# A two-block transformer layer in float32: GpSimd work, modulation products, transposes and three steps of the second block rearranged

## The chip, the cores and the metric

The kernel runs on one core of a Trainium2 chip. A core has five engines that work side by side, each through its own queue in order: TensorE (PE in the profile; PEld is its weight load), VectorE (DVE), ScalarE (ACT), GpSimd (POOL) and SyncE (SP), which only issues transfers. The metric is the device time of one execution in microseconds (us); lower is better.

## The reference

Batch 1, 512 tokens, width 1024. A first block, then a second, each once; all float32.

```python
def first_block(x, c, ...):
    mod = silu(c) @ w_mod + b_mod                       # 6 x 1024 columns
    sh1, sc1, gt1, sh2, sc2, gt2 = split(mod, 6)
    h = rms_norm(x, g_norm1) * (1 + sc1) + sh1
    q, k, v, ga, gb = split(h @ w_in)                   # 5 x 512 columns
    attn = dilated_attention(q, k, v)                   # 8 heads of 64, softmax
    u = ga * sigmoid(gb)
    y = causal_depthwise_conv(u, conv_w, width=31) + conv_b
    conv = silu(layer_norm(y, conv_ln_g, conv_ln_b))
    x = x + gt1 * (concat(attn, conv) @ w_out)
    h2 = rms_norm(x, g_norm2) * (1 + sc2) + sh2
    x = x + gt2 * hier_moe(h2, ...)                     # 32 experts, top 2 of a group
    return rms_norm(x, g_final)

def second_block(x, meta, ...):                         # 16 meta tokens ahead: 528 rows
    hn = rms_norm(h); sb_q, sb_k, sb_v, g_q, g_k, g_v, g_r, g_lr, merge = split(hn @ w_in)
    sb = stick_breaking(sb_q, sb_k, sb_v)               # 8 heads of 64
    g = log_sigmoid(g_lr @ w_gk_up + b_gk) / 16         # g_lr: 16 columns
    o = rms_norm(gla(g_q, g_k, g_v, g)) * silu(g_r)     # 4 heads, chunked recurrence
    mix = (gate_sb * (sb @ w_sb_out) + gate_gla * (o @ w_gla_out)) @ w_o
    h = h + rms_norm(mix)
    h = h + rms_norm((gelu(conv3(rms_norm(h) @ w_up)) * (rms_norm(h) @ w_gate)) @ w_down)
```

## The kernel before

**Weights.** One stream (`Stream`, L225) brings every weight matrix of both blocks through a plan of units of up to 1 MB, in the order of their use. SP issues a unit's transfer (L271) as soon as one of its `raw` buffers is free: four in the first block until the attention ends, then six more. A buffer is free when its last reader is done with it, and the transfers leave SP in the order of the plan. A unit that is used in the fast product is cast in chunks of 1024 or 512 columns to a high and a low part, `whi` and `wlo` (`split`, L219): ACT rounds the chunk (L220), and VectorE subtracts (L221). For the first 20 chunks (`LOP`, L223 and L479), which are those of `w_gab`, `w_v` and `w_qk`, GpSimd does the subtraction. Three chunks are cast ahead of use. A product of two split operands is three matmuls (`mm3`, L308: L309 to L311).

**Modulation.** The 6144 columns of `mod` come in 24 units of 256 columns (`mod_gen`, L497). A unit's weights lie with the output columns on the partitions, and VectorE multiplies them by silu(c) and sums along the row in one instruction for each 128 columns (L523), two to a unit, then adds `b_mod` (L502). Three units, 15, 21 and 23 (`NMP`), are multiplied on GpSimd (L519), summed by ACT (L507) and get their bias on GpSimd. Units 0 to 7 are used two at a time for the norm of the input (`normed1`, L556), two come after each odd step of the value projection, one after each odd query-key product, four in the attention (`MA`) and four in the output projection.

**First block in order.** (1) The gate projection `pg` with the norm woven in, up to `u = ga * sigmoid(gb)` (L599). (2) The value projection `pv` (L646 to L658), four steps with one chunk each. (3) Eight query-key products `p` (`qk_proj`, L663), the first head pair's attention woven in. (4) Attention over four head pairs (`hp`) of four row blocks (`i`), in a software pipeline: scores `pqk` (L686), bias and maximum on VectorE (L695), exponential on ACT (L699), a diagonal matrix of 1/sum (`dg`, L708, on ACT), a product `pt` of scores and `dg` that transposes and scales at once (L712), its copy `pT` (L720), and the values `pso` (L729), which are split into `mh` and `ml`. (5) All along, VectorE works on the convolution: 120 taps `y = u * w + y` of 128x512 (L633, L635), issued four at a time (`taps`) at a lower priority, so that they stand between the other VectorE work wherever the list scheduler of the framework puts them. Four more taps are products on TensorE (`pe_taps`, `pyt` L859), added by L861. (6) First halves of the output projection `pw` on the attention's half of the rows, the convolution's layer norm (`conv_norm`, `psl`, `psl2`, L824 to L847) woven in, then the second halves on the convolution's rows. (7) Router, and the mixture of experts.

**Second block, the three places.** `proj2_gen` (L1579) multiplies a cast 128-column weight with `nh` and `nl`, the two parts of the normed input, in two column halves of 264. Of `g_lr` only 16 columns exist; their weights come as a 128-column unit, cast like the rest, and make `pl` in 48 matmuls (L1712). In the stick-breaking part (L1745 to L1880) a pipeline of 40 units (4 head pairs `hp`, 5 key blocks `j`, 2 heads `b`) begins with the scores `pz` of one head (`sb_z`, L1783), a contraction over 64 rows of which the other head uses the other 64; it is woven with the query-key projections `pq` (L1587) and the linear attention's levels `pat`. `Sums` (L1612) sums squares over the partitions for the two norms behind: each square is multiplied into one of four 32-row groups of a bank (L1633), ACT copies the bank (L1640), and a second product adds the groups up (L1641).

The order on each engine is made by a list scheduler from the order in which the program is written, with priorities where `high_priority` says so; it was read from the compiled program.

## Time and profile before

| | |
|---|---|
| median of 3 runs | 1839.62 us (1836.7, 1839.62, 1840.88) |
| the profiled execution, its own time | 1838.8 us |
| span of the trace | 1837.0 us, 1.8 us less than its time |
| mean granted TensorE clock | 0.976 of full speed |
| busy in the span: PE, DVE, ACT, POOL | 1752.8, 923.4, 626.5, 180.4 us |
| first block up to the second halves of the output projection | 0 to 257.7 us |
| stick-breaking and linear attention, with their projections | 883 to 1047 us |

A slice of the page's strips is 1/40 of the span, 46 us, and a digit is the busy share in tenths. In the table of windows each row gives, for one stretch, its length and for each engine the busy time and the number of instructions, then the granted clock (1.00 is 2.4 GHz, 0.50 is 1.2 GHz), the share of the 16 transfer engines and GB/s. In the rows by line the numbers behind the bar are the busy time of the group in us, the mean duration of one instruction in ns, and the idle time of the engine just before them with what ended it. An fp32 matmul is two records in the trace, one of split operands is one; matmuls are pipelined, so that the durations of neighbours overlap.

### The profile page before, as it was taken

How to read it: one execution, taken by the hardware profiler on the slowest of the kernel's cores; microseconds unless marked ns; L12 is line 12 of the kernel's file. 1: busy time of each engine (PE TensorE's matmuls, PEld its weight loads, DVE VectorE, ACT ScalarE, POOL GpSimd, SP SyncE). 2: the span in 40 equal slices, each digit the busy share in tenths (PEclk: the TensorE clock that was granted, in tenths of full speed). 3: DMA queues.
4: the chain of work that ended last, by engine and by line, in shares of the span. 5: the costliest groups of instructions: out<-in, count | busy, mean ns of one | idle time of the engine just before them, and what ended most of it. 6: DMA issues, size and time to landing. Idle time of an engine off the chain costs nothing.

```text
span 1837.0 us, 26718 instructions
## 1 busy us (share of the span) xinstructions
PE 1752.8 (95%) x10738; PEld 1264.7 (69%) x10738; DVE 923.4 (50%) x1593; ACT 626.5 (34%) x1146; POOL 180.4 (10%) x162
## 2 busy tenths in 40 slices
PE   6978987999999999999999999999999999999997
PEld 4755754544445444445888768989999799889985
DVE  7999864542424343335577752253331654335534
ACT  3324653211111111104566663252223633223322
POOL 4541020000000000004100000030000111001101
PEclk9998998999999999999999999999999999999998
DMA  8743163899999999941411012113222122232221
GB/s 300 283 165 134 73 231 127 303 409 409 408 411 377 371 407 409 413 166 38 157 63 47 25 38 101 47 50 136 104 95 91 46 92 93 90 105 93 92 86 63
DMA packets 73889, 328.29 MB, mean 179 GB/s; under 512 B 7971, under 2 KB 8227, under 8 KB 59556
## 3 DMA queue, kind: packets, MB, share of 16 engines
q1 hardware_dynamic: 72608, 320.75, 46.3%
q0 software_dynamic: 1152, 5.81, 0.9%
q8 instruction: 85, 1.39, 0.3%
q14 instruction: 40, 0.33, 0.1%
q10 hardware_dynamic: 4, 0.00, 0.0%
HBM read 322.27 MB, written 4.26 MB: 178 GB/s over the span
## 4 chain that ended last, share of the span: by engine, by line
PE 50%; DVE 2%; ACT 1%; POOL 1%; issue 0%; DVEq 0%; ACTq 0%; POOLq 0%
PE p L1609 11%; PE pup L2210 7%; PE pq L1587 6%; PE pg L311 2%; PE pg L309 2%; PE pg L310 2%; PE pd L310 2%; PE pd L311 2%; PE pd L309 2%; PE pz L1789 1%; PE pv L309 1%; PE psb L1870 1%; PE pv L311 1%; PE pv L310 1%; PE pmix L309 1%; PE pmix L310 1%
## 5 line engine op out<-in xcount | busy, mean ns | idle before, releaser
L221 DVE TENSOR_TENSOR wsplit<-raw,wsplit 128x1024 fp32r<-128x1024 f32 (+1 forms) x140 | 166.8, 1194 | 258.5 <-ACT wsplit L220 253.0
L220 ACT ACTIVATE wsplit<-raw 128x1024 fp32r<-128x1024 f32 (+1 forms) x145 | 147.9, 1022 | 261.8 <-PE pd L311 76.4
L1195 PE MATMUL pgu<-raw,x 128*64 128x512 f32 x960 | 220.3, 598 | 0.0
L1195 PEld LDWEIGHTS pgu<-raw,x 128*64 128x64 f32 x960 | 64.1, 136 | 120.0 <-issue 106.9
L1288 DVE SCALAR_TENSOR_TENSOR x<-psx,modc,x 128x512 f32<-128x512 f32 x136 | 93.1, 744 | 48.1 <-PE psx L1296 48.0
L1237 DVE SCALAR_TENSOR_TENSOR yl<-pdn,wsl,yh 128x512 fp32r<-128x512 f32 x34 | 25.4, 751 | 178.8 <-ACT yh L1236 178.4
L1195 PE MATMUL pdn<-raw,hT 128*64 128x512 f32 x480 | 105.7, 593 | 0.7 <-ACT hT L1217 0.7
L635 DVE SCALAR_TENSOR_TENSOR y<-u,cpk,y 128x512 f32<-128x512 f32 x116 | 103.3, 924 | 0.4
L1217 ACT ACTIVATE hT<-pht 128x512 f32<-128x512 f32 x17 | 10.2, 598 | 232.1 <-PE pht L1211 227.5
L1195 PEld LDWEIGHTS pdn<-raw,hT 128*64 128x64 f32 x480 | 34.5, 137 | 69.1 <-issue 64.4
L310 PE MATMUL pd<-wsplit,ah 128*128 128x512 f32 x176 | 71.0, 403 | 2.1 <-DVE wsplit L221 2.0
L1157 PE MATMUL psg<-oh,h2h 128*128 128x256 f32 (+1 forms) x288 | 68.9, 297 | 3.2 <-DVE oh L1142 3.2
L311 PE MATMUL pd<-wsplit,al 128*128 128x512 f32 x176 | 70.0, 398 | 0.0
L309 PE MATMUL pd<-wsplit,ah 128*128 128x512 f32 x176 | 69.1, 398 | 1.0 <-ACT wsplit L220 1.0
L1609 PE MATMUL p<-nha,wsplit 128*128 128x258 f32 x384 | 68.6, 291 | 1.0 <-ACT grb L2059 0.6
L1157 PE MATMUL psg<-oh,h2l 128*128 128x256 f32 (+1 forms) x288 | 65.7, 281 | 0.0
L1609 PE MATMUL p<-nhb,wsplit 128*128 128x258 f32 x384 | 65.5, 282 | 0.0
L221 POOL TENSOR_TENSOR wlo<-raw,whi 128x1024 fp32r<-128x1024 f32 x20 | 59.4, 2982 | 57.7 <-ACT whi L220 47.2
L2210 PE MATMUL pup<-nha,wsplit 128*128 128x258 f32 x352 | 63.9, 290 | 0.9 <-ACT wsplit L220 0.9
L523 DVE CUSTOM_DVE_ANT_0 raw<-raw,h 128x1024 f32<-128x1024 f32 x38 | 62.4, 1668 | 1.1 <-DMA raw<-w_mod 1.1
L1295 PE MATMUL psx<-ohT,yh 128*128 128x512 f32 x136 | 59.3, 436 | 3.3 <-ACT uh L1455 3.0
L2210 PE MATMUL pup<-nhb,wsplit 128*128 128x258 f32 x352 | 61.4, 284 | 0.0
(649 smaller groups left out, 4050.7 us busy)
## 6 DMA issues: line engine op xcount, KB each, us to landing
raw<-w_moe SPq DMA_DIRECT2D x312, 512.0 KB, 10.1
raw<-w_moe SPq DMA_DIRECT2D x36, 1024.0 KB, 8.9
raw<-w_mod SPq DMA_DIRECT2D x24, 1024.0 KB, 6.4
raw<-w_ff SPq DMA_DIRECT2D x22, 1024.0 KB, 4.8
raw<-w_qk SPq DMA_DIRECT2D x12, 1024.0 KB, 4.9
raw<-w_v SPq DMA_DIRECT2D x8, 1024.0 KB, 4.9
raw<-w_mg SPq DMA_DIRECT2D x8, 1024.0 KB, 4.8
raw<-w_fd SPq DMA_DIRECT2D x8, 1024.0 KB, 4.8
```

The costliest lines, as they stand in the source:

```text
L220: act(hi, src, AF.Copy)
L221: return sub(lo, src, hi.bitcast(F32), OP.subtract)
L309: mm(ps, lh, rh, start=first, stop=False)
L310: mm(ps, lh, rl, start=False, stop=False)
L311: mm(ps, ll, rh, start=False, stop=last)
L635: tap[0] = stt(y[:, m, :], src, w, y[:, m, :], OP.mult, OP.add)
L1157: fix(mm(ps[k // 2][:, k % 2 * 256:][:, :n], w[i][:, k * P:(k + 1) * P], oh[:, i, :n], start=(i == 0 and w is h2h and k % 2 == 0), stop=(i ...
L1195: fix(mm(ps[s, :], l[:, s], w[:, 2 * b + i, :], start=first, stop=last, skip_group_check=True))
L1288: stt(xT[m], ps, gt2(m), xT[m], OP.mult, OP.add)
L1587: mm(ps[a], l[:, kk, :], r[kk][:, a * HF:(a + 1) * HF], start=(kk == 0 and fl == 0), stop=(kk == k - 1 and fl == 2))
L1609: mm(ps[a], l[:, kk, :], ends(r[kk])[:, a], start=(kk == 0 and fl == 0), stop=(kk == k - 1 and fl == 2))
L2210: mm(ps[:, a, :HC], l[:, kk, :], x[kk][:, o:o + HC], start=(kk == 0 and fl == 0), stop=(kk == KD - 1 and fl == 2))
```

## The change

In the first block:

- `LOP` goes: all 20 low parts are subtracted on VectorE.
- `NMP` goes: no unit is multiplied on GpSimd, and units 21 and 23 are VectorE's.
- Units 8 to 15 (`MPE`) become products on TensorE. Their weights (`w_modk`) lie with the contraction on the partitions; eight fp32 matmuls of 32 equal columns of silu(c) (`ccols`, made by GpSimd at the start) against 256 columns fill four 32-row groups of a bank, ACT copies them (`evm`), and two matmuls against 1/32 (`part32`) add up groups and copies to a column, to which VectorE adds `b_mod` (`mod_columns`). Four units are used behind the second and four behind the fourth step of the value projection, none in the query-key products. A raw buffer of theirs is free when TensorE has read it.
- `at_transpose`: ACT scales the scores in place by 1/sum, n = 128 to 512 columns, and TensorE transposes them with its transpose operation; `dg` goes.

In the second block:

- `g_lr`: the weights come uncast as 32 columns for each of the 8 row blocks, 32 fp32 matmuls fill four 32-row groups, and `wgk`, zero between its four copies, adds the groups up in the product that follows.
- `sb_z` takes two banks at the first head and issues the scores of both heads behind each other.
- `Sums`: a square is summed by one matmul with 128 columns of ones as soon as the next product is issued; the copy and the second product go.

```diff
...
@@ -287 +288 @@
-                    i = split(hi, lo, src, nc.gpsimd.tensor_tensor if self.nc in LOP else self.lo)
+                    i = split(hi, lo, src, self.lo)
@@ -384,0 +386,7 @@
+    ccol = early.tile([P, KD], F32, name="ccol")
+    act(ccol, cc("c", 0, KD), AF.Silu)
+    ccols = early.tile([P, KD, 32], F32, name="ccols")
+    for k in range(KD):
+        nc.gpsimd.tensor_scalar(ccols[:, k, :], ones[:, 0:32], ccol[:, k:k + 1], None, OP.mult)
+    part32 = early.tile([P, 2], F32, name="part32")
+    nc.vector.memset(part32, 1.0 / 32)
@@ -394 +402 @@
-    NMP = (15, 21, 23)
+    MPE = range(8, 16)
@@ -407 +415 @@
-            add(I["w_mod"][2 * j + h], (2048,), False)
+            add(I["w_modk"][2 * j + h - 12] if 6 <= j < 10 else I["w_mod"][2 * j + h], (2048,), False)
@@ -414 +422 @@
-        add_mod(2)
+        add_mod(4)
@@ -417 +424,0 @@
-        add_mod(1)
...
@@ -499,12 +502 @@
-        late, crow = [], crow_h2
-        def done(c, eng):
-            eng.tensor_tensor(modc[:, c:c + 2], macc[:, c:c + 2], cc("b_mod", c, 2), OP.add)
-        def sums():
-            for raw, c in late:
-                for b in range(2):
-                    act(raw[:, b, :], raw[:, b, :], AF.Copy, accum_out=macc[:, c + b:c + b + 1])
-                done(c, nc.gpsimd)
-            late.clear()
+        crow = crow_h2
@@ -512,3 +503,0 @@
-            with tc.high_priority(offset=-100):
-                sums()
-            raw = ws.nxt(D)
@@ -515,0 +505,14 @@
+            mod_columns()
+            if n in MPE:
+                raw = ws.nxt(256)
+                ps = p1("pmod")
+                for k in range(KD):
+                    g = 32 * (k % 4)
+                    mm(ps[g:g + 32, 0:256], ccols[:, k, :], raw[:, k, :], start=(k < 4), stop=(k >= 4),
+                       skip_group_check=True)
+                ev = big.tile([P, T], F32, name="evm", tag="t512", bufs=2)
+                act(ev[:, 0:256], ps[:, 0:256], AF.Copy)
+                rows_of.append((ps, ev, c))
+                yield
+                continue
+            raw = ws.nxt(D)
@@ -518,8 +521,4 @@
-            if n in NMP:
-                nc.gpsimd.tensor_tensor(raw, raw, crow[:, None, :].to_broadcast([P, 2, D]), OP.mult)
-                late.append((raw, c))
-            else:
-                for b in range(2):
-                    nc.vector.tensor_tensor_reduce(raw[:, b, :], raw[:, b, :], crow, 1.0, 0.0, OP.mult, OP.add,
-                                                   macc[:, c + b:c + b + 1])
-                done(c, nc.vector)
+            for b in range(2):
+                nc.vector.tensor_tensor_reduce(raw[:, b, :], raw[:, b, :], crow, 1.0, 0.0, OP.mult, OP.add,
+                                               macc[:, c + b:c + b + 1])
+            tt(modc[:, c:c + 2], macc[:, c:c + 2], cc("b_mod", c, 2), OP.add)
...
@@ -529,0 +528,11 @@
+    rows_of = []
+    def mod_columns():
+        for ps, ev, c in rows_of:
+            for b in range(2):
+                mm(ps[:, 256 + 2 * b:258 + 2 * b], ev[:, b * P:(b + 1) * P], part32, start=True, stop=True,
+                   skip_group_check=True)
+            tt(modc[:, c:c + 2], ps[:, 256:260:2], cc("b_mod", c, 2), OP.add)
+        rows_of.clear()
@@ -657,2 +666,2 @@
-            next(mod)
-            next(mod)
+            for _ in range(4):
+                next(mod)
@@ -669,2 +677,0 @@
-            if i % 2:
-                next(mod)
@@ -706 +713 @@
-        dg = big.tile([P, 2, P], F32, name="dg", tag="dg", bufs=2)
+        n = (i + 1) * P
@@ -708 +715 @@
-            act(dg[:, b, :], ident, AF.Copy, scale=sm[:, 6 + b:7 + b])
+            act(s[:, b, :n], s[:, b, :n], AF.Copy, scale=sm[:, 6 + b:7 + b])
@@ -712 +719 @@
-                mm(pt[b][:, j * P:(j + 1) * P], s[:, b, j * P:(j + 1) * P], dg[:, b, :], start=True, stop=True)
+                transpose(pt[b][:, j * P:(j + 1) * P], s[:, b, j * P:(j + 1) * P], ident)
...
@@ -1632,3 +1640 @@
-                g, k = self.n[a] % 4, self.n[a]
-                mm(self.ps[a][32 * g:32 * g + 32], ones[:, 0:32], part(sq, a), start=(k < 4), stop=(k >= 4),
-                   skip_group_check=True)
+                mm(self.ps[a], ones, part(sq, a), start=(self.n[a] == 0), stop=(self.n[a] == KD - 1))
@@ -1639,4 +1645 @@
-            ev = t5("ev")
-            act(part(ev, a), self.ps[a], AF.Copy)
-            mm(self.ps[a], ones, part(ev, a), start=True, stop=True)
-            tc.keep_in_program_order(act(part(r, a), self.ps[a], AF.Ln, bias=epsb, scale=1.0 / (32 * count)))
+            tc.keep_in_program_order(act(part(r, a), self.ps[a], AF.Ln, bias=epsb, scale=1.0 / count))
@@ -1712,2 +1715,8 @@
-    for i, _ in enumerate(proj2_gen(KD, nh, nl, pl)):
-        if i == 2:
+    w = ws.nxt(32)
+    for k0 in (0, 4):
+        for x in (nh, nl):
+            for a in range(2):
+                for k in range(4):
+                    mm(pl[a][32 * k:32 * k + 32], w[:, k0 + k, :], x[k0 + k][:, a * HF:(a + 1) * HF].bitcast(F32),
+                       start=(k0 == 0 and x is nh), stop=(k0 > 0 and x is nl), skip_group_check=True)
+        if k0 == 0:
...
@@ -1722,2 +1731,4 @@
-    wgk = cp.tile([16, 512], F32, name="wgk")
-    nc.gpsimd.dma_start(wgk, I["w_gk_up"])
+    wgk = cp.tile([P, 512], F32, name="wgk")
+    nc.gpsimd.memset(wgk, 0.0)
+    for g in range(0, P, 32):
+        nc.gpsimd.dma_start(wgk[g:g + 16], I["w_gk_up"])
@@ -1782,0 +1794,2 @@
+    pz = {}
@@ -1783,0 +1797 @@
@@ -1785,6 +1799,10 @@
-        need(("s", hp))
-        s0, t0, n = SBT[j]
-        ps = p1("pz")
-        r, p = slice(64 * b, 64 * b + 64), sb_keys(j)
-        mm(ps[:p, :n], skh[hp][r, s0:s0 + p], sqh[hp][r, t0:t0 + n], start=True, stop=True)
-        return ps
+        if b == 0:
+            need(("s", hp))
+            s0, t0, n = SBT[j]
+            p = sb_keys(j)
+            for h in range(2):
+                pz[h] = p1("pz")
+            for h in range(2):
+                r = slice(64 * h, 64 * h + 64)
+                mm(pz[h][:p, :n], skh[hp][r, s0:s0 + p], sqh[hp][r, t0:t0 + n], start=True, stop=True)
+        return pz.pop(b)
@@ -2166,0 +2185 @@
+            su.flush(a)
@@ -2169,2 +2187,0 @@
-            if m in (3, 5):
-                su.flush(a)
@@ -2174,0 +2192 @@
+            su.flush(a)
@@ -2196,0 +2215 @@
+            su.flush(a)
@@ -2198 +2217 @@
-            if k % 2:
+            if k == KD - 1:
```

Three places in the order of the engines. The first is SP's queue of weight transfers from the value projection's first unit on (`w_v`, two units; `w_qk`, four; `w_mod` and `w_modk` are modulation units), with what each waits for; before:

```order
L271 DMA raw<-w_v 128x2048 [waits DMAHW7_49,Pool_49]
L271 DMA raw<-w_mod 128x2048 [waits DMAHW0_49,DVE_49]
L271 DMA raw<-w_mod 128x2048 [waits DMAHW1_49,DVE_49]
L271 DMA raw<-w_v 128x2048 [waits DMAHW2_49,Pool_49]
L271 DMA raw<-w_mod 128x2048 [waits DMAHW4_49,DVE_49]
L271 DMA raw<-w_qk 128x2048 [waits DMAHW5_49,DVE_49]
L271 DMA raw<-w_mod 128x2048 [waits DMAHW3_49,Pool_49]
L682 DMA strip<-strip 128x2x512
L271 DMA raw<-w_qk 128x2048 [waits DMAHW7_49,DVE_49]
```

and now:

```order
L272 DMA raw<-w_v 128x2048 [waits DMAHW7_49,DVE_49]
L272 DMA raw<-w_modk 128x2048 [waits DMAHW0_49,DVE_49]
L272 DMA raw<-w_modk 128x2048 [waits DMAHW1_49,DVE_49]
L272 DMA raw<-w_modk 128x2048 [waits DMAHW2_49,DVE_49]
L689 DMA strip<-strip 128x2x512 x2
L272 DMA raw<-w_modk 128x2048 [waits DMAHW3_49,DVE_49]
L272 DMA raw<-w_v 128x2048 [waits DMAHW4_49,PE_49]
L272 DMA raw<-w_modk 128x2048 [waits DMAHW5_49,PE_49]
L272 DMA raw<-w_modk 128x2048 [waits DMAHW6_49,PE_49]
L272 DMA raw<-w_modk 128x2048 [waits DMAHW1_49,PE_49]
L272 DMA raw<-w_modk 128x2048 [waits DMAHW2_49,DVE_49]
L272 DMA raw<-w_qk 128x2048 [waits DMAHW7_49,DMAHW3_49,PE_49]
```

The second `w_v` unit stood two modulation units behind the first and waited for GpSimd; it now stands four behind it and waits for TensorE to have read a modulation unit. The `w_qk` units, of which the last row shows the first, do so too.

The second is VectorE behind the last scores of the attention, up to the sum of the taps from TensorE (L861, now L869): taps (L635, now L644), modulation units (L523, now L522, each with a read of its sum), the last part of the attention (`ml`) and the low parts of the first three `w_out` chunks (`wlo`). Before:

```order
L705 RECIPROCAL sm<-sm 128x2
L635 SCALAR_TENSOR_TENSOR y<-u,cpk_67,y 128x512 x6
L221 TENSOR_TENSOR ml<-pso,mh 128x512
L635 SCALAR_TENSOR_TENSOR y<-u,cpk_67,y 128x512 x3
L221 TENSOR_TENSOR wlo<-raw,whi 128x512
L635 SCALAR_TENSOR_TENSOR y<-u,cpk_67,y 128x512 x3
L221 TENSOR_TENSOR wlo<-raw,whi 128x512
L635 SCALAR_TENSOR_TENSOR y<-u,cpk_67,y 128x512 x2
L221 TENSOR_TENSOR wlo<-raw,whi 128x512
L523 ISA raw,macc<-raw,u 128x1024
L523 ISA macc 128x1
L861 TENSOR_TENSOR y<-pyt,y 128x512
```

and now:

```order
L712 RECIPROCAL sm<-sm 128x2
L524 TENSOR_TENSOR modc<-macc,cpk_67 128x2
L224 TENSOR_TENSOR ml<-pso,mh 128x512
L224 TENSOR_TENSOR wlo<-raw,whi 128x512
L522 ISA raw,macc<-raw,u 128x1024
L522 ISA macc 128x1
L224 TENSOR_TENSOR wlo<-raw,whi 128x512
L522 ISA raw,macc<-raw,u 128x1024
L522 ISA macc 128x1
L224 TENSOR_TENSOR wlo<-raw,whi 128x512
L524 TENSOR_TENSOR modc<-macc,cpk_67 128x2
L869 TENSOR_TENSOR y<-pyt,y 128x512
```

Of 18 taps behind the last scores, the last 14 of which stand in the rows of before, two are left, ahead of the rows of now; two modulation units stand there instead, one ahead of `ml` (its bias is the second row), the other with one instruction ahead of the second low part and one ahead of the third.

The third is TensorE where the scores of the stick-breaking part with 400 columns begin (`pz` from `sqk`; `psb` are values, `pz` from `sp` sums of an earlier unit). Before:

```order
L1870 MATMUL psb<-z,sv 64x16 [waits Activation_49]
L1870 MATMUL psb<-z,sv 64x16
L1837 MATMUL pz<-sp,mtge 128x144 [waits DVE_49]
L1841 MATMUL pz<-sp,mones 128x16
L1789 MATMUL pz<-sqk 128x400 [waits DVE_49]
L1587 MATMUL pq<-nha,wsplit 128x264 x2
```

and now:

```order
L1888 MATMUL psb<-z,sv 64x16
L1855 MATMUL pz<-sp,mtge 128x144
L1859 MATMUL pz<-sp,mones 128x16
L1807 MATMUL pz<-sqk 128x400 [waits Activation_49]
L1807 MATMUL pz<-sqk 128x400 [waits DVE_49]
L1595 MATMUL pq<-nha,wsplit 128x264 x2
```

The two heads' scores stand next to each other, and each waits for its own bank.

## Rows read from the trace of the kernel before

**Rows 1.** The page's strips, 40 slices: busy tenths of PE, granted clock.

```profile
PE   6978987999999999999999999999999999999997
...
PEclk9998998999999999999999999999999999999998
```

**Rows 2.** Windows: start:end, length, PE, PEld, DVE, ACT, POOL, clock, DMA share, GB/s.

```profile
0.00:73.00 73.00, 57.80 (x215) 40.11 (x216) 59.70 (x82) 26.54 (x34) 37.89 (x28) 0.95 0.77 284
73.00:95.40 22.40, 22.40 (x97) 18.02 (x97) 22.37 (x35) 5.14 (x5) 12.47 (x5) 1.00 0.75 281
95.40:165.20 69.80, 55.42 (x222) 41.43 (x222) 69.80 (x108) 21.07 (x43) 22.68 (x8) 0.88 0.47 170
165.20:212.00 46.80, 40.15 (x307) 28.99 (x306) 45.09 (x126) 32.52 (x101) 1.56 (x1) 0.93 0.13 46
...
221.40:257.70 36.30, 29.52 (x108) 19.72 (x108) 30.49 (x39) 17.87 (x29) 9.85 (x4) 0.91 0.73 282
883.00:1047.00 164.00, 162.63 (x1830) 134.52 (x1830) 107.72 (x222) 103.58 (x223) 9.26 (x15) 0.99 0.20 68
```

**Rows 3.** Waits of PE, 0 to 330 us: total, times, longest.

```profile
PE p L309 <- ACT whi L220: 8.9, 1, 8.9
PE psl L824 <- DVE y L861: 6.8, 1, 6.8
...
PE pt L712 <- ACT dg L708: 5.0, 3, 3.7
```

**Rows 4.** The page's groups of instructions, three of them.

```profile
L221 DVE TENSOR_TENSOR wsplit<-raw,wsplit 128x1024 fp32r<-128x1024 f32 (+1 forms) x140 | 166.8, 1194 | 258.5 <-ACT wsplit L220 253.0
...
L221 POOL TENSOR_TENSOR wlo<-raw,whi 128x1024 fp32r<-128x1024 f32 x20 | 59.4, 2982 | 57.7 <-ACT whi L220 47.2
...
L523 DVE CUSTOM_DVE_ANT_0 raw<-raw,h 128x1024 f32<-128x1024 f32 x38 | 62.4, 1668 | 1.1 <-DMA raw<-w_mod 1.1
```

**Rows 5.** Groups of DVE by line: taps at 0 to 138, then at 185 to 222.

```profile
L635 DVE SCALAR_TENSOR_TENSOR y<-u,cpk,y 128x512 f32<-128x512 f32 x36 | 35.8, 1046 | 0.0
...
L635 DVE SCALAR_TENSOR_TENSOR y<-u,cpk,y 128x512 f32<-128x512 f32 x34 | 24.7, 746 | 0.2
```

**Rows 6.** DVE in order of time behind the attention: start, duration, instruction, count.

```profile
215.16 4.67 DVE L635 SCALAR_TENSOR_TENSOR y<-u,cpk,y 128x512 f32<-128x512 f32 x6
...
226.15 6.50 DVE L635 SCALAR_TENSOR_TENSOR y<-u,cpk,y 128x512 f32<-128x512 f32 x3
...
233.17 5.80 DVE L635 SCALAR_TENSOR_TENSOR y<-u,cpk,y 128x512 f32<-128x512 f32 x2
...
240.63 0.68 DVE L861 TENSOR_TENSOR y<-pyt,y 128x512 f32<-128x512 f32 x1
...
243.60 1.21 DVE L523 CUSTOM_DVE_ANT_0 raw<-raw,u 128x1024 f32<-128x1024 f32 x1
```

**Rows 7.** Weight transfers issued at 190 to 262 us: count, KB, us to landing.

```profile
raw<-w_mod SPq DMA_DIRECT2D x3, 1024.0 KB, 7.6
```

**Rows 8.** Weight transfers of the whole execution, from the page: count, KB, us to landing.

```profile
raw<-w_qk SPq DMA_DIRECT2D x12, 1024.0 KB, 4.9
```

**Rows 9.** PE in order of time: a burst of sums of squares, a second product.

```profile
1397.38 1.53 PE L1633 MATMUL psum<-sq,ones 128*32 128x260 f32 x16
...
1420.55 0.67 PE L1641 MATMUL psum<-ev,ones 128*128 128x260 f32 x2
```

**Rows 10.** Groups of ACT by line, 165 to 222 us.

```profile
L720 ACT ACTIVATE pT<-pt 128x384 f32<-128x384 f32 (+3 forms) x28 | 11.9, 445 | 9.3 <-PE pt L712 9.2
L708 ACT ACTIVATE dg<-ident,sm 128x128 f32<-128x128 f32 x26 | 9.0, 393 | 2.4 <-DVE sm L697 1.8 <-DVE sm L705 0.5
```

**Rows 11.** Groups of PE by line: scores at 95 to 222, then at 883 to 1047.

```profile
L686 PE MATMUL pqk<-qk 64*128 64x128 f32 (+3 forms) x64 | 14.0, 494 | 0.0
...
L1789 PE MATMUL pz<-sqk 64*16 64x16 f32 (+4 forms) x62 | 21.2, 421 | 0.6 <-ACT sqk L1758 0.6
```

**Rows 12.** One matmul group of `pl`: durations, first and last start.

```profile
L1587 PE MATMUL pl<-nhb,wsplit x16: 280/284/288, 875.2 to 880.9; 128*128 128x264 f32 x16
```

More of the change, by code (lines that the diff above doesn't have):

```diff
@@ L35 @@
     ("b_mod", 48), ("g_norm1", 8), ("conv_b", 4), ("conv_ln_g", 4), ("conv_ln_b", 4),
-    ("conv_w", 4 * 31), ("g_norm2", 8), ("w_router", 8 * 36),
+    ("conv_w", 4 * 31), ("g_norm2", 8), ("w_router", 8 * 36), ("c", 8),
     ("g_final", 8), ("norm_mix_pre", 8), ("b_gk", 4), ("gla_head_norm", 2),
@@ L67, in pack_inputs @@
     wr = np.concatenate([f("w_router_group")[0], f("w_router_expert")[0]], axis=1)
+    parts["c"] = col(f("c"))
     parts["w_router"] = wr.reshape(8, P, 36).transpose(1, 0, 2).reshape(P, 288)
@@ L97, in pack_inputs @@
         "w_mod": wm.T.reshape(24, 2, P, D).transpose(0, 2, 1, 3).reshape(24, P, 2 * D),
+        "w_modk": np.stack([wm[:, (2 * j + h) * 256:(2 * j + h + 1) * 256].reshape(KD, P, 256).transpose(1, 0, 2)
+                           .reshape(P, 2048) for j in (6, 7, 8, 9) for h in range(2)]),
         "c_row": f("c").reshape(1, D),
@@ L107, in pack_inputs @@
         "w_v2": pair(np.concatenate([rows(w2[:, c:c + 512], 2) for c in (1024, 2560, 3072)])),
-        "w_lr": cols(w2, [4608]),
+        "w_lr": np.pad(w2[:, 4608:4624], ((0, 0), (0, 16))).reshape(KD, P, 32).transpose(1, 0, 2).reshape(1, P, KD * 32),
         "w_qk2": pair(cols(w2, [c + h * P for c, h in (
@@ L221, in split @@
         return sub(lo, src, hi.bitcast(F32), OP.subtract)
-    LOP = []
     class Stream:
@@ L460, in _build @@
     plan += [(I["w_v2"][i], two, "keep") for i in range(2)]
-    plan += [(I["w_lr"][0], (1024,), True)]
+    plan += [(I["w_lr"][0], (KD * 32,), False)]
     plan += [(I["w_qk2"][i], two, True) for i in range(8)]
@@ L476, in _build @@
     ws = Stream(plan, castp, 3, nmoe)
-    for u, (_, sizes, cast) in enumerate(plan[:nmoe]):
-        if cast:
-            LOP.extend(range(ws.first[u], ws.first[u] + len(sizes)))
-    del LOP[20:]
     for h in range(2):
@@ new lines, in mod_gen @@
+        for n, (j, h) in enumerate(mod_order):
+            c = 4 * j + 2 * h
+            mod_columns()
[11 more added lines that the diff above has]
+                continue
@@ L526, in mod_gen @@
+            tt(modc[:, c:c + 2], macc[:, c:c + 2], cc("b_mod", c, 2), OP.add)
             yield
-        sums()
         yield
+    rows_of = []
[6 more added lines that the diff above has]
+        rows_of.clear()
     mod = mod_gen()
@@ L744, in _build @@
     qkp = qk_proj()
-    for _ in range(2):
-        next(qkp)
+    next(qkp)
+    mod_columns()
+    next(qkp)
     wr = lambda k: cc("w_router", 36 * k, 36)
@@ L1711, in _build @@
     pl = [p("pl")[:, :HF] for p in (pns, psx)]
-    for i, _ in enumerate(proj2_gen(KD, nh, nl, pl)):
-        if i == 2:
+    w = ws.nxt(32)
[6 more added lines that the diff above has]
+        if k0 == 0:
             sv_last()
     tc.keep_in_program_order(nc.scalar.preload_act_table_set("natural_log_exp_and_others"))
-    glr = t5("glr", 16)
+    glr = t5("glr")
     for a in range(2):
-        act(glr[:, a * HF:(a + 1) * HF], pl[a][0:16], AF.Copy)
+        act(glr[:, a * HF:(a + 1) * HF], pl[a], AF.Copy)
     ws.lo = tt
```

1 line of the change is left out of this document (removed).

## Prediction

> **What bounds the kernel now.** The page's strips come first: from the seventh slice on PE has nines nearly throughout, so behind 276 us the kernel is PE's work, and only the first six slices, about 276 us, have holes [rows 1]. The windows then cut the first block at the ends of its stages [rows 2]. In 0 to 73 (the gate projection) PE is busy 57.8 of 73.0 us. From 73 on VectorE is the full engine: 22.37 of 22.40 in the value projection, 69.80 of 69.80 in the query-key products, 45.09 of 46.80 until the last scores at 212.0, while PE is busy 55.42 of 69.80 and 40.15 of 46.80 there. The waits of PE name what VectorE and GpSimd hold up: 8.9 us for the cast of a weight, 5.0 for `dg`, and 6.8 behind the attention for the convolution's sum `y` [rows 3]. The granted clock falls to 0.88 and 0.93 in the stretches with those waits. In the second block the place of the change is PE-bound: 162.63 of 164.00 us busy at 883 to 1047, with VectorE at 107.72 and ACT at 103.58 [rows 2], so there each microsecond that PE no longer needs is one of the span, as long as neither fills up.
>
> Times below are of the profiled execution, 1838.8 us, which lies 0.8 under the median of the runs.
>
> **First block, up to the values.** GpSimd took 2.98 us for a low part that VectorE does in 1.19 [rows 4]. In the gate projection the eight low parts come sooner, and PE needs 11.2 us for each of its four steps (half of the value projection's 22.40 us, at full clock, since both have 96 products of 512 columns [rows 2] and a step of `pg` has 48). By the order two of the first four modulation instructions now stand behind the first normed row, which waits for the norm, rather than ahead of it, so the first product comes some 2.7 us later (2 x 1.21 us [rows 6] and a table load), at about 22.7, and four steps with the slow clock at the start end near 71, 2 us earlier than before.
>
> VectorE's account from there to the last scores (139.0 us before): gone are units 8 to 14, seven units of two instructions at 1.668 us [rows 4], 23.4 us, and what taps lose while GpSimd works, 36 x (1.046 - 0.746) = 10.8 us [rows 5]. New are twelve low parts at 1.194, 14.3 us, and 16 taps (18 behind the last scores become 2) at 24.7 / 34 = 0.73, 11.6 us. That is 8.3 us less: if VectorE never waited, the last scores would end at 212.0 - 2 - 8.3, near 201.5.
>
> A rule of the Trainium skill would make that floor lower. The page "SBUF — State Buffer", section "Who interferes with whom", has VectorE and GpSimd share one port pair as an exclusive lock, so that the loser stands still for the whole of the other's instruction; by it all of GpSimd's 12.47 + 22.68 = 35.2 us in these two stretches would come back. The rows show instead that a tap beside GpSimd takes 1.4 times its time [rows 5]. With the rule VectorE would be done so early that PE alone would set the end, which is the second rival below with more chance.
>
> PE's account to the last query-key product (165.2 before): 22.4 + 55.42 x 0.88 = 71.2 us of old work at full clock. The waits for the cast and most of that for `dg` go with GpSimd. New are eight units on PE: eight products of 260 columns in four row groups take 1.53 us [rows 9]; with the two small products and the hand-over to ACT I take 1.9, so 15.2 us (12.2 if all but the burst is hidden, 20 if it waits for ACT in full). New too is that the second value unit and the query-key units can only be fetched when PE has read a modulation unit: the transfer takes 4.9 us [rows 8], cast and low part 2.2 more (the low part may stand behind four taps, 2.9), and three units on PE, 5.7 us, cover it. That leaves 1.4 to 4.3; I take 4 for each of the two places, since a tap is always ready on VectorE. The half clock that follows either costs perhaps 1 to 2 us. From 71: 71 + 71.2 + 15.2 + 8 = 165.4, about 166: **the query-key products gain nothing**, and VectorE waits for them.
>
> **Attention and tail.** Between the last query-key product and the last scores VectorE has five taps fewer by the order (28 for 33 in the last three head pairs), 3.7 us; ACT scales 26 times up to 512 columns where it made 128x128 at 0.393; the nearest row, a copy of the same widths, has 0.445 [rows 10], so ACT's 32.5 of 46.8 us grow by 1.4, or by 4.5 at worst if in place costs as the exponential does, and stay under VectorE. So the last scores come at 166 + 46.8 - 3.7 = 209 to 210, and the last values 8.4 later (9.4 before; the transposes are one record for two), at 218: 3.5 us earlier than before. The tail to the second halves was 36.3 us. Taps beside GpSimd took 6.50 us for three and 5.80 for two there, and `y` was summed only at 240.63 [rows 6]; now two taps stand behind the last scores, so the wait of 6.8 us [rows 3] goes, and of the slow clock (0.91 of 29.5 busy us [rows 2]) 2.7 us. What is late next: unit 21, whose weights are fetched when the attention frees its pool. Three such transfers took 7.6 us in the median, the first of them some 5 [rows 7, 8]. The unit's first instruction now stands ahead of the second chunk's low part, which so comes 5 + 1.2 + 0.7 = 6.9 us after the last values, while PE is through with the first chunk after about 4: a new wait of 3 us (0 to 5). The tail is 36.3 - 6.8 - 2.7 + 3 = 29.8. The second halves start at 218 + 29.8, near 248 for 257.7: **10 us gained in the first block**. This passes on, since the transfers of the experts' weights also start from the pool that the attention frees. Ends: a gain of 21 if VectorE runs to its floor and unit 21 is hidden; a loss of 3 if the units cost 20 us, attention keeps its pace and the wait is 6.
>
> **Second block.** Scores in pairs: the attention's scores have the same form with both heads together: 64 records (32 products of 320 columns on average) in 14.0 us, 1.37 ns a column; the lone scores show 62 of their 80 records in 21.2 us, so 27.4 for 40 products of 269 columns on average, 2.55 ns a column [rows 11]. At the pairs' rate they take 14.7 us, 12.7 less. Each pair now needs two banks at once and by the order waits for ACT and VectorE there, so I take **11.5**, with 8 and 14 as ends. VectorE, at 107.72 of what would be 152 us, doesn't fill up. `g_lr`: 48 products from 873.7 to 881.2, 7.5 us (a quarter of them starts in 875.2 to 880.9 [rows 12]); now four bursts of eight, 4 x 1.53 = 6.1 [rows 9], and no cast on ACT and GpSimd ahead: **2**, ends 0 and 3.5, because the input's last parts arrive when they do. `Sums`: four copies and four second products of 0.67 us [rows 9] go, half of them in a chain that PE waits for, some 3 us; squares that stood in bursts of four groups now cost a full-width product each, where the bursts were few: **2**, ends -2 and 4. Together 15.5, with 8 and 20 as ends.
>
> Sum: 1838.8 - 10 - 15.5 = 1813.3.
>
> **The rivals.** *First: the first block gains nothing.* PE is behind VectorE once the units are on it, and each wait is followed by half clock (0.88 where it waits now [rows 2]). The query-key products then end near 172, attention follows, and the tail only gets back what they lost: 1838.8 - 15.5 = 1823. For it speaks that PE's sum, 165.4, has no slack against 165.2; against it, that 14.4 us of idle PE time stand in the window now. *Second: VectorE's floor.* If low parts are seldom behind taps, the two waits shrink to 1.4, the last scores come near 202 and the gain is 20: 1803. *Third, slower: the clock.* PE's old work from 73 to 257.7 is about 144 us at full clock (the busy times of rows 2 times their clocks, with 8.5 at 212 to 221.4). Now about 12 us of it are lost at half clock. More and shorter pauses (units that wait for ACT, transposes half as long) could leave PE at 1.2 GHz through most of the attention; each microsecond of work there costs another. It decides from 12 + 25.5 = 38 us of work at half clock on; at 50 the time is 1838.8 - 25.5 + 50 - 12 = 1851. Against it: the attention's window is at 0.93 now with the same small products. *Fourth: pairs don't run side by side*, because the second waits for its bank. Then the second block gives 4, the sum is 1825; with the first rival too, 1835.
>
> **How the numbers follow.** Forecast 0.57 (1804 to 1821), first rival 0.17 (1819 to 1829), second 0.13 (1797 to 1805), fourth 0.05 (1821 to 1828), first and fourth together 0.03 (1831 to 1838), slower 0.05. The time is the forecast's, 1813. The range leaves out the slower case, the double one and the lower half of the second: 1800 to 1828. A measurement of this kernel tells about 0.2%, 3.7 us, from no change: faster 0.91, within it 0.04 (most of the double case and of the small losses), slower 0.05.
>
> **What would show it.** Right: no tensor work on POOL at 73 to 258; taps at 0.75 us throughout; waits of PE of about 4 us ahead of the fifth chunk half of `pv` and of the first `p`; the last scores at 205 to 213; no wait of `psl` for `y`, but one of `pw` for a low part; second halves at 244 to 252; a pair of 512-column scores in about 1.1 us and the stretch from 883 shorter by 8 to 14. Wrong: `p` ending after 170, clock under 0.8 in the attention, waits of `pz` for ACT above 0.3 us each.

## The result

The changed kernel takes 1823.82 us in the median of five runs (1819.1 to 1827.15), before 1839.53; the ratio is 0.9918, with a 95% interval of 0.9902 to 0.9934. That is 15.7 us (12 to 18) less, where 25.5 were forecast (1813) and the range went to 1828. The traced run took 1819.83 us, near the lower end of the five, with a span of 1818.0 for 1837.0, so that the two traces differ by 19.0 us, 3 more than the medians. Of those 19.0 the first products of the experts (`psg`) come 11.2 us earlier, and the rest lies in the second block.

### The profile page after: what moved, and what is told of

Read it like the earlier page. It is cut to its first block, busy times and chain, and to the rows that moved or that the text cites. A ratio compares the mean times of both kernels' runs of the same rounds, so it can differ in the third digit from the quotient of the medians.

```text
span 1818.0 us, 26874 instructions
## 1 busy us (share of the span) xinstructions
PE 1740.4 (96%) x10826; PEld 1258.9 (69%) x10826; DVE 882.1 (49%) x1597; ACT 628.6 (35%) x1141; POOL 109.9 (6%) x147
## 4 chain that ended last, share of the span: by engine, by line
PE 48%; DVE 4%; ACT 2%; DMA 1%; POOL 1%; issue 0%; DVEq 0%; ACTq 0%; POOLq 0%
PE p L1617 11%; PE pup L2229 7%; PE pq L1595 4%; PE pg L312 2%; PE pg L310 2%; PE pg L311 2%; PE pd L311 2%; PE pd L312 2%; PE pd L310 2%; PE pv L310 1%; PE pv L312 1%; PE pv L311 1%; PE pmix L310 1%; PE pmix L312 1%; PE pmix L311 1%; PE psb L1888 1%
## 5 line engine op out<-in xcount | busy, mean ns | idle before, releaser
L644 DVE SCALAR_TENSOR_TENSOR y<-u,cpk,y 128x512 f32<-128x512 f32 x116 | 81.4, 750 | 0.1
L1165 PEld LDWEIGHTS psg<-oh,h2h 128*128 128x128 f32 x288 | 54.0, 198 | 9.7 <-issue 5.7
L1617 PEld LDWEIGHTS p<-nha,wsplit 128*128 128x128 f32 x384 | 56.3, 195 | 3.0 <-ACT wsplit L223 0.9
```

What stands on the lines that cost most here:

```text
L644: tap[0] = stt(y[:, m, :], src, w, y[:, m, :], OP.mult, OP.add)
L1165: fix(mm(ps[k // 2][:, k % 2 * 256:][:, :n], w[i][:, k * P:(k + 1) * P], oh[:, i, :n], start=(i == 0 and w is h2h and k % 2 == 0), stop=(i ...
L1617: mm(ps[a], l[:, kk, :], ends(r[kk])[:, a], start=(kk == 0 and fl == 0), stop=(kk == k - 1 and fl == 2))
```

## The profile after

The windows of [rows 2], with the same cuts and columns, in the changed kernel:

```profile
0.00:73.00 73.00, 59.35 (x224) 41.46 (x225) 49.11 (x100) 31.87 (x41) 12.27 (x26) 1.00 0.81 299
73.00:95.40 22.40, 18.04 (x125) 12.53 (x124) 18.38 (x32) 3.54 (x6) 0.00 (x0) 0.93 0.49 184
95.40:165.20 69.80, 66.09 (x319) 48.56 (x318) 61.71 (x111) 24.33 (x46) 2.30 (x2) 0.92 0.53 186
165.20:212.00 46.80, 41.34 (x276) 25.32 (x274) 42.52 (x121) 37.46 (x104) 0.00 (x0) 0.96 0.14 46
212.00:221.40 9.40, 7.86 (x62) 6.42 (x63) 2.78 (x7) 4.80 (x11) 0.00 (x0) 1.00 0.48 143
221.40:257.70 36.30, 36.30 (x142) 24.02 (x141) 23.55 (x43) 19.28 (x32) 4.64 (x16) 1.00 0.76 304
```

GpSimd (the last of the five busy times) has left 73 to 95 us altogether, but VectorE, full there before, is now idle for 4.0 of 22.40 us, and for 8.1 of the next 69.80. The waits of PE up to 330 us, for [rows 3]:

```profile
PE pmod L534 <- ACT evm L514: 3.2, 7, 0.5
...
PE pva L311 <- DVE wlo L224: 2.3, 1, 2.3
...
PE pt L719 <- ACT s L715: 1.7, 3, 1.1
PE p L312 <- DVE wlo L224: 1.7, 1, 1.7
```

The waits of 8.9 for a cast and 6.8 for `y` are gone. New are those of the units and two for a low part, of the third weight chunk of the values (its first half is the fifth of all halves) and of the first query-key chunk. VectorE's own waits at 71 to 215 us show what it is idle for:

```profile
DVE modc L536 <- PE pmod L534: 10.0, 8, 3.2
```

It stands 10.0 us before the eight additions of `b_mod`, each of which needs a unit's last product from PE. PE in order of time at the first group of four units (start, duration, instruction, records, wait):

```profile
81.98 1.50 PE L511 MATMUL pmod<-raw,ccols 128*32 128x256 f32 x22
83.63 0.61 PE L534 MATMUL pmod<-part,evm 128*128 128x2 f32 x4 [0.15 <-ACT evm L514]
84.17 1.07 PE L511 MATMUL pmod<-raw,ccols 128*32 128x256 f32 x16
85.69 0.61 PE L534 MATMUL pmod<-part,evm 128*128 128x2 f32 x4 [0.45 <-ACT evm L514]
...
91.00 0.50 PE L310 MATMUL pva<-whi,hh 128*128 128x512 f32 x1 [0.45 <-ACT whi L223]
93.98 0.80 PE L311 MATMUL pva<-wlo,hh 128*128 128x512 f32 x1 [2.25 <-DVE wlo L224]
```

Four units take from 81.98 to 90.54, 2.14 us each, and then the next chunk is not cast. Its weights are not what is late: their transfer was issued at 83.19 and took 4.8 us. ACT rounds the chunk right behind the last unit's copy, from 89.89 on, and VectorE, which follows the order of its own queue, subtracts behind three taps:

```profile
90.72 2.06 DVE L644 SCALAR_TENSOR_TENSOR y<-u,cpk,y 128x512 f32<-128x512 f32 x3
92.71 2.36 DVE L224 TENSOR_TENSOR wlo<-raw,whi 128x1024 fp32r<-128x1024 f32 x2
```

The second group, 107.17 to 115.77, ends in the same way. The waits for casts are 2.7 us behind the first group (0.45 and 2.25) and 2.0 behind the second (0.34 and 1.68), and the clock falls behind each. Windows of 10 us of the changed kernel; between 100 and 110 us, and from 130 to 190 us, the clock is 1.00:

```profile
90.00:100.00 10.00, 7.29 (x22) 5.48 (x23) 9.36 (x15) 1.89 (x2) 0.00 (x0) 0.66 0.83 319
110.00:120.00 10.00, 6.43 (x51) 3.23 (x43) 7.18 (x14) 3.98 (x6) 0.67 (x1) 0.82 0.99 383
120.00:130.00 10.00, 10.00 (x37) 8.02 (x38) 8.91 (x12) 1.55 (x2) 0.00 (x0) 0.84 0.40 134
```

PE is busy for some 10.5 us at 1.2 GHz there, so about half of that, 5.3 us, is lost (an estimate from these records). The query-key products end at 169.9, for 165.2 before; the last scores at 210.1, for 212.0; the last values at 219.0, and the second halves begin at 246.5, for 257.7.

## The experiments

Each is the changed kernel but for its edit, if nothing else is said, and is compared by its ratio to the kernel before; a difference of two such ratios is known to about 0.25%, 4 to 5 us.

**The two halves apart.** `first_only` has the second block of before, `second_only` the first block of before.

> The change's first-block half alone, the second block as before. Prediction's sum: 10 us less than before. By the two traces (the experts' first products came 12 us earlier): 12 us less, and everything behind 320 us as before. Rival (the gain sits in the second block, the first only looks earlier): under 6 us.

> The three changes of the second block alone, the first block as before. Prediction's sum: 15.5 us less than before (scores in pairs 11.5, gate weights 2, sums 2). By the two traces: 7 us less, of which the sums 4.5, the scores 4.7, and the start of the second block loses 2 at the end of the experts. Rival (the profiled run of the changed kernel lost its half of the gain to a slower clock only): 12 us or more.

Measured: 0.9977 (0.9961 to 0.9992), 4 us less than before, and 0.9953 (0.9935 to 0.9972), 9 less; together 13 of the 15.7. The first half's 4 us is in the rival's range (under 6), but not for the rival's reason: in its trace the experts' first products do come 9.8 us earlier (308.3 for 318.1). The second half's 9 lies between the 7 read from the traces and the 12 of its rival. The first half is worth less than forecast and than its own trace says (1827.85 for 1838.8): its ten runs spread from 1827.11 at a clock of 0.986 to 1839.43 at 0.975. So it was traced again.

> The first-block half alone once more, for a second trace: its runs spread from 1827 to 1839 us, and the time goes with the mean granted clock (0.986 to 0.975), while its first trace was of the run at 1828. If the spread is that of half-clock stretches, a run near 1835 shows some more of them (about 7 us of lost clock, each of 3.4) and the same work in the same order; if this run is also near 1828, the place stays open. Rival (the spread is in the experts' transfers): the same clock, and the experts' stretch longer.

This run took 1833.58 us at 0.978. Windows of the two traces, first run, then second:

```profile
190.00:230.00 40.00, 34.77 (x215) 23.10 (x216) 26.88 (x70) 26.80 (x68) 0.00 (x0) 0.96 0.30 112
```

```profile
190.00:230.00 40.00, 35.02 (x174) 23.43 (x174) 21.24 (x60) 22.89 (x60) 0.00 (x0) 0.69 0.16 55
```

PE is busy as long in both, but gets through 174 instructions for 215, at a clock of 0.69 for 0.96: the end of the attention and the tail ran mostly at 1.2 GHz, and the convolution's last part (`ml` from `y`) ended at 255.7 for 247.2. The experts' stretch kept its length, which speaks against the rival. So the same program, with the same work, reaches the experts' first products 8.3 us later in one run than in the other (316.6 for 308.3), from one place where PE waits often; 2.6 of it come back in the second block, and 5.7 are left in the time. The second trace is 0.7 us from the median of the ten, the first 6.4.

**The low parts back on GpSimd.** `LOP` holds the first 20 chunks again, as before:

```diff
-                    i = split(hi, lo, src, self.lo)
+                    i = split(hi, lo, src, nc.gpsimd.tensor_tensor if self.nc in LOP else self.lo)
```

> The changed kernel with the first 20 low parts on GpSimd again (2.98 us each for 1.19). If the first block's gain is mostly this part's: 6 us or more longer, taps at 1.0 us while GpSimd works, and the 8.9 us wait for a cast ahead of a query-key product is back. Rival (the gain is that of the products on TensorE and the tail): within 3 us of the changed kernel, since VectorE has 24 us less to do.

Measured: 1843.49 us, 1.0033 (1.002 to 1.0046), 21 us more than the changed kernel and slower than before. Taps at 73 to 138 us take 931 ns on average (755 in the changed kernel), `u` ends 6.8 us later and the query-key products 14.3 later. The wait of 8.9 us for a cast did not come back, as had been expected: PE waits 1.5 us twice for GpSimd's low parts, and 6.6 and 4.7 us for ACT in the attention, where the clock is 0.78 at 165.2 to 212 us (0.96 in the changed kernel). In this kernel, with the units in fours, this part alone is worth more than the whole first half; others of it must cost.

**The units on VectorE; the units on PE, but not in fours.** The first edit empties `MPE` and puts units 8 to 15 back to their places of before; the second keeps them on PE and only changes places and transfers:

```diff
     for i in range(2):
         add(I["w_v"][i], (1024, 1024))
-        add_mod(4)
+        add_mod(2)
     for i in range(4):
         add(I["w_qk"][i], (1024, 1024))
+        add_mod(1)
...
-            for _ in range(4):
+            for _ in range(2):
                 next(mod)
...
             taps(4)
+            if i % 2:
+                next(mod)
             yield
```

> The changed kernel with units 8 to 15 on VectorE at their places of before (two behind each second value step, one behind each second query-key product), nothing on GpSimd. If VectorE is what ends the attention: its eight units of 2.4 us put the last scores 10 us or more later (210 to 220), the time 8 to 10 us longer. Rival (TensorE's query-key products, 170 for 165 us, end it, held up by the units and by the transfers behind them): the products end 8 or more earlier, the time is the same or shorter.

> The changed kernel with units 8 to 15 still products on TensorE, but used at their places of before (two behind each second value step, one behind each second query-key product), and their transfers in that order. If what they cost in the changed kernel (11 us against VectorE at those places) is the grouping in fours, with the wait for the next weights behind each group (3.4 and 2.0 us) and VectorE idle meanwhile: the query-key products end near 158, and the time is 8 us or more under the changed kernel's, near 1813. Rival (it is TensorE's time for the units, 8 x 2.25 us): the query-key products end near 165 and the time is at most 4 us under.

Measured: 1812.24 us, 0.986 (0.9844 to 0.9876), for VectorE, 11 us less than the changed kernel; and 1801.81 us, 0.9805 (0.9786 to 0.9824), for PE with the units spread, 21 less. The first is the rival's outcome (the products end earlier, and the time is shorter), the second that of the theory of the grouping. So what costs is neither PE's time for the units nor the engine, but the places of the units, four in a row, with their transfers ahead of the next weights. Places and transfers were changed together; which of them counts was not tried, and in the trace above the transfer of the third value chunk had landed before ACT came to it. With the units spread (in twos in the value projection, singly in the query-key products) VectorE's wait for them is

```profile
DVE modc L537 <- PE pmod L535: 3.6, 7, 0.8
```

and PE's windows (the second ends with the query-key products at 154.3, 15.6 us earlier) have hardly a hole and the full clock, with seven of the eight units in them; the eighth follows the last product, which makes some 2 of the 15.6 us. The others are what the groups cost: PE's waits for ACT's copies (0.2 us for 3.2), those for casts (4.7, gone) and the half clock behind them (5.3, gone):

```profile
71.40:96.90 25.50, 25.34 (x135) 19.65 (x134) 23.99 (x44) 5.89 (x7) 0.00 (x0) 1.00 0.51 183
96.90:154.30 57.40, 57.26 (x318) 42.60 (x316) 54.48 (x107) 24.20 (x49) 2.24 (x2) 1.00 0.60 210
```

The query-key products end 4 us ahead of what the theory of the grouping expected (158) and 11 ahead of its rival (165).

With all units on VectorE they end at 143.6 (this trace is of the slowest of the four runs, 1818.33 us; the others took 1811.15 to 1813) and the last scores come at 182.2, 28 us earlier than in the changed kernel; but the taps are then behind the attention, and PE waits for them:

```profile
PE psl L835 <- DVE y L872: 9.7, 1, 9.7
```

**Diagonals and products in place of scaling and transposes.**

> The changed kernel with the diagonal matrices and products in place of the scaling and the transposes, as before. If transposes pay as forecast (last values 1 us sooner, TensorE's 80 products at half the records): 1 to 3 us longer than the changed kernel. Rival (the shorter work of TensorE only lets its clock fall more often in the attention): the same or shorter, with the clock at 1.00 in 190 to 230.

Measured: 1818.5 us, 0.9891 (0.9874 to 0.9908), 5 us less than the changed kernel, about what can be told; its four runs lie within 4 us, the changed kernel's five within 8. ACT's scaling in the changed kernel at 170 to 222 us, and the transposes of both at 95 to 222 (of the changed kernel, then with products):

```profile
L715 ACT ACTIVATE s<-s,sm 128x512 f32<-128x512 f32 (+3 forms) x26 | 13.5, 567 | 3.9 <-DVE sm L712 3.8
```

```profile
L719 PE MATMUL pt<-ident,s 128*128 128x128 f32 x80 | 13.6, 294 | 1.8 <-ACT s L715 1.7
```

```profile
L719 PE MATMUL pt<-dg,s 128*128 128x128 f32 x160 | 22.1, 284 | 0.8 <-ACT dg L715 0.8
```

The transposes save PE 8.5 us, but in a stretch where it isn't the bound: with products the window 190 to 230 has it busy 38.45 of 40.00 us at a clock of 1.00. ACT pays 0.567 us for each scaling where a diagonal cost 0.393 [rows 10], as much as the exponential (0.564 in the same window of before) and not as a copy (0.445). In the two traces the changed kernel is still 1.8 us ahead (spans 1818.0 and 1819.8), so the loss lies in the runs that were not traced: of those the changed kernel's four have a mean clock of 0.975 to 0.980, the three with products 0.982 or 0.983. That the clock can fall in this attention is shown for `first_only`, which has the same one; that these runs lose it there, the rival's reason, is not shown.

**One head's scores at a time.**

> The changed kernel with the scores of one head at a time, as before. If the pairs are worth the 13 us of TensorE time that they save: 13 us more than the changed kernel. By the traces, where the stretch from the first pq product to the last psb product is only 4.7 to 7 us shorter: 5 us more. Rival (pairs cost as much as they save, by waits for their banks): the same time as the changed kernel.

Measured: 1827.23 us, 0.9941 (0.9921 to 0.9961), 4 us more. The scores on PE at 872 to 1037 us of the changed kernel:

```profile
L1807 PE MATMUL pz<-sqk 64*16 64x16 f32 (+4 forms) x68 | 11.3, 409 | 2.3 <-ACT sqk L1769 2.3
```

For 68 of 80 records 11.3 us, 13.3 for all: 14 less than the 27.4 of before [rows 11], so the pairs do run side by side, and PE saves what was forecast. From the first `pq` product to the first state of the linear attention (`pS`) it is 250.1 us for 254.9 without pairs (254.8 before). Two windows show where the rest of the 14 us goes. The first begins with the first `pq` product and holds the same work, before, then after:

```profile
883.70:1053.60 169.90, 168.41 (x1922) 137.73 (x1922) 113.46 (x236) 108.67 (x239) 9.26 (x15) 0.99 0.18 63
872.80:1035.50 162.70, 157.78 (x1919) 133.94 (x1920) 112.60 (x237) 104.94 (x237) 11.63 (x22) 0.99 0.21 73
```

PE is busy for 10.6 us less, since neighbours overlap, but idle for 3.4 more, and the stretch is 7.2 us shorter. Of the idle time 1.7 us is a wait for `sqk` (2.3 us for 0.6 before). It isn't the pairs': without pairs it is 1.7 us, and with pairs and the old gate weights 0.6. The second window, the end of it, holds the same 598 records, before, after, and in `second_only`:

```profile
1035.60:1095.80 60.20, 58.79 (x598) 36.84 (x598) 37.92 (x87) 41.93 (x96) 1.57 (x4) 1.00 0.05 19
1018.30:1080.10 61.80, 58.67 (x598) 36.87 (x598) 37.73 (x86) 42.06 (x94) 3.11 (x4) 0.94 0.05 18
1029.90:1088.60 58.70, 55.57 (x598) 35.37 (x598) 37.76 (x86) 41.99 (x94) 3.11 (x4) 1.00 0.06 19
```

At the full clock it is 1.5 us shorter than before, in the traced run of the changed kernel, at 0.94, 1.6 longer. `second_only` does the whole stretch up to `pS` in 246.3 us, 8.5 less than before.

**The gate weights and the sums as before.**

> The changed kernel with the gate weights cast and multiplied 128 columns wide, as before. If the 2.0 us that TensorE now waits longer at the end of the experts (5.1 us for a cast, 3.0 us for uh before) come from the cast order that the missing cast shifts: that wait is back at 3 us and pl takes 7.5 us again, no difference in time. Rival (that wait has another cause): it stays at 5.1 us and the time is 2 us longer.

> The changed kernel with the sums of squares in four row groups, their copy and second product, as before. By the prediction 2 us more than the changed kernel. By the traces, where the clock stays full at 1412 to 1446 us (it was at half for 6.8 us at 1430) and the first up product to the last took 4.5 us less: 5 us more, with the half clock back at that place.

Measured: 1822.49 us, 0.9924 (0.9907 to 0.9941), no difference, and 1825.99 us, 0.9934 (0.9907 to 0.9961), 3 us more, inside what can be told. `pl` does take 5.7 us for 7.6, but the next `pq` starts 3.5 us behind it for 2.5, and the wait for `sqk` behind that is 2.3 us for 0.6: what the gate weights save comes back as waits. The wait at the end of the experts stays at 5.1 us with the old gate weights, so my theory on it falls; it is in the trace of `first_only` too and not in that of `second_only` (3.0), so it comes with the first half, and why stays open. The full-width sums cost PE more than the groups, 18.9 us at the two norms for 13.1 and 2.4 of the second products in the run with the old sums; if they gain, it is by what no longer follows them. The half clock of before at 1430 did not come back with the old sums (1.00 at 1417 to 1451 us), as I had expected it to.

**Better than both.** With all units on VectorE, PE waits 9.7 us for taps; ten more taps are given to it:

```diff
-    NPT = 4
+    NPT = 14
```

> Units on VectorE at their places of before (the kernel at 1812), and 14 of the 124 taps on TensorE rather than 4. There VectorE is full to 232 us and TensorE waits 9.7 us for y at 0.75 of its clock. If VectorE's taps set the second halves: y comes 10 x 0.67 = 6.7 us sooner, 1806. Rival (the ten products of 0.86 us stand ahead of the sum over y on TensorE and their diagonals on ACT): 1811 or more.

Measured: 1796.33 us, 0.9771 (0.9752 to 0.9789), 43 us under before and 16 under the same kernel with 4 taps, where 6.7 were expected. Windows of the tail with 4 taps, then with 14:

```profile
181.00:226.00 45.00, 31.45 (x149) 21.07 (x148) 42.26 (x70) 12.50 (x25) 0.00 (x0) 0.88 0.51 195
226.00:245.00 19.00, 13.57 (x36) 8.16 (x37) 12.98 (x27) 10.81 (x16) 6.68 (x16) 0.59 0.48 187
```

```profile
181.00:226.00 45.00, 43.48 (x189) 28.27 (x188) 42.54 (x75) 23.82 (x46) 0.00 (x0) 1.00 0.59 228
226.00:245.00 19.00, 19.00 (x75) 10.90 (x74) 10.30 (x19) 8.95 (x18) 7.09 (x16) 1.00 0.50 166
```

The ten products take PE's idle time, its wait for `y` is gone, and the clock, at 0.88 and 0.59, is full. The taps' own time on VectorE, 6.7 us, is less than half of the gain; the clock is the other thing that differs. How much of the 16 us it is stays open: the trace with 4 taps is of a run 6 us above the median of its kernel, at a mean clock of 0.975 where the other three have 0.980, so it shows more of the half clock than they had. Letting the last units stand behind the mean's subtraction changed nothing, which is the rival's outcome:

> The same, with units 20 to 23 allowed on VectorE only behind the subtraction of the mean (L839), so that three of their instructions no longer stand between the sum of the taps and it. If those 3.6 us are on the path to the second halves: 3 us less than the kernel with 14 taps, 1803. Rival (the subtraction waits for TensorE's sum anyway, and the experts' first transfers now come later behind the units' buffers): the same or slower.

Measured: 1796.65 us, 0.9777 (0.9758 to 0.9796).

## Why the prediction was right, and where it was off

- *The number*: 1823.82 lies in the range, but above the forecast's own band (1804 to 1821), where the first rival (1823) and the fourth (1825) stand. Neither of them happened: the first block gained 4 us and not nothing, the second 9 and not 15.5, and the pairs do run side by side. The mechanisms of the forecast were right and two of its sizes were about twice too large; that the range held the time it owes to the room made for rivals, and so far it is luck.
- *Low parts off GpSimd* (right in kind, low in size): the forecast gave VectorE 8.3 us on balance. Its busy time at 73 to 212 us fell by 14.7, from 137.3 to 122.6 (the windows of [rows 2] and of the profile after), and undoing this part costs 21 us. The term that was too small is what VectorE loses beside GpSimd; the last paragraph of this section shows why. Taps fell to 755 ns as said. `pg` ended at 70.9, near 71 as said, but by two errors that cancel: its first product came at 24.5 us for 22.7, and the slow clock at its start did not come (1.00 at 0 to 73 us).
- *Units on PE: "the query-key products gain nothing"* (right): forecast 166, measured 169.9, 4.7 us later than before (165.2). The units take 17.1 us (8 x 2.14) for 15.2, since each waits for ACT's copy of its own bank. The waits for casts came to 2.7 and 2.0 us for 4 and 4, with the low part behind three taps as forecast. The half clock behind the waits cost some 5.3 us; the forecast put it at 1 to 2 for each, but took only 0.6 into its sum. With these sizes the sum is 71 + 71.2 + 17.1 + 4.7 + 5.3 = 169.3: the term that was too small is the clock. The forecast saw the waits and took the placing as given; spreading the units gives back 21 us, and it didn't ask what the same units cost elsewhere.
- *Attention*: last scores at 210.1 (209 to 210), last values 219.0 (218), and ACT's scaling at the worst of its two bounds, 0.567 us (0.445 taken, 0.564 the end).
- *Tail*: 27.5 us for 29.8; unit 21's weights came 0.4 us late for VectorE, and no low part was waited for, though a wait of `pw` for one was named as a sign.
- *First block in sum*: 11 us in the trace (10), but 4 (1.5 to 7) over the runs. The difference is the third rival's mechanism, not strong enough for its sign: in the attention PE's pauses are such that the clock fell in one of two traced runs (0.69 at 190 to 230 us) and hardly in the other (0.96). I had put it down as all or nothing.
- *Pairs* (11.5 forecast): the mechanism and PE's saving were right (14 us of its time), the step to the span wasn't, which took every saved microsecond of PE as one of the span: PE was idle for 3.4 us more, and 4.8 us arrived in the stretch, 4 in the time. The end that I gave, 8, was too high. Of the signs, the stretch came out 4.8 us shorter and not 8 to 14, and a wait of `pz` for ACT above 0.3 us, named as a sign of being wrong, came (2.3 us), though with the gate weights.
- *Gate weights* (2): nothing; PE saves 1.9 us on them and waits as much longer behind. *Sums* (2): about that, 3, within the noise.

On the rule of the Trainium skill weighed ahead (the page "SBUF — State Buffer", section "Who interferes with whom", an exclusive lock): the trace of the kernel before bears it out, and the forecast misread its rows when it said that a tap beside GpSimd takes 1.4 times its time. That is a mean. Of the 36 taps in [rows 5], 30 took 0.73 to 0.74 us, one 1.16, and five 2.83 to 2.90. It is not the taps alone: nearly each low part on GpSimd holds one VectorE instruction for about 2.1 us, whatever its size. Three low parts of before, and VectorE beside them:

```profile
34.50 8.85 POOL L221 TENSOR_TENSOR wlo<-raw,whi 128x1024 fp32r<-128x1024 f32 x3 [6.24 <-ACT whi L220]
35.37 3.38 DVE L523 CUSTOM_DVE_ANT_0 raw<-raw,h 128x1024 f32<-128x1024 f32 x1
38.79 2.22 DVE L502 TENSOR_TENSOR modc<-macc,cpk 128x2 f32<-128x2 f32 x1
41.05 2.32 DVE L561 SCALAR_TENSOR_TENSOR a<-modc,cpk 128x2 f32<-128x2 f32 x1
```

The product and sum of L523 took 1.22 us alone, the additions of two columns 0.15 to 0.22. At 73 to 212 us such holds add up to some 25 us (an estimate: each record less its time alone). The forecast counted 17 of it, 10.8 for taps and 6.3 within the mean of the units (14 x (1.668 - 1.22)). By the rule as weighed it would be 35.2; in these rows a hold is about 2.1 us of the 2.98, not all of it. So VectorE had some 8 us more room than the forecast gave it, and PE alone set the end of the query-key products, as it said would follow from the rule.

## What to carry to other kernels

Work that is moved to an idle engine should stand singly or in twos, with other work of both engines between: the same eight units, with their weights fetched ahead of the next product's, cost 21 us more in groups of four. Read single records and not only means beside a second engine: a mean of 1.05 us for 0.75 was a few instructions held for 2.1 us each. A gain of engine time in a stretch where that engine isn't the bound can bring nothing, and pauses can cost clock: the two traces of `first_only` show that, and the loss by transposes, 5 us, is at the edge of what can be told. Filling a pause with another engine's work gained more than that work's time in the one case tried. One trace of one run is not enough where runs of a kernel spread by 12 us: look at each run's clock.

## What the runs showed that was not expected

The same program's runs lie 12 us apart (1827 to 1839) and follow the mean granted clock (0.986 to 0.975); kernels whose first block leaves PE few pauses spread less and have a higher clock (1799.96 to 1803.67 us at 0.985 to 0.986 with the units spread, 1794.31 to 1797.12 at 0.986 to 0.987 with 14 taps). Few pauses are not the only way to a small spread: `second_only`, with the first block of before, lies at 1827.5 to 1831.23 us, at 0.974 to 0.977. Moving 10 taps of 0.67 us from a full VectorE to a waiting PE gained 16 us, 9 more than their time on VectorE.
